# Attention in a two-layer encoder: head outputs in their own tile, causal entries by a select, bias rows loaded a head ahead

## The chip, the cores and the metric

The kernel runs on one core of a Trainium2 chip. The core has a matrix engine (TensorE, "PE" in the profile, with its weight loads shown apart as "PEld"), a vector engine (VectorE, DVE), a scalar engine (ScalarE, ACT), a general engine (GpSimd, POOL) and a sync engine (SP), which here does nothing but issue DMA transfers. Each engine works through a queue of its own in order, and the engines meet through semaphores. The metric is the device time of one execution in microseconds (us), as the median of several runs.

## The reference: what is computed

Two layers over 512 tokens of width 1024, in f32. Each layer adds to x a SwiGLU feed-forward, then a mixer, then a second feed-forward, each behind a norm with shift, scale and gate from a vector c. The mixer has three branches, and two of them are attention with eight heads of dimension 64:

```python
# branch A (group "a"): chunked, with a learned bias by clipped distance
logits = jnp.where(valid, logits + bias, NEG_INF)
# branch C (group "c"): frame-causal, with a forgetting bias
logits = einsum('bqhd,bkhd->bhqk', qb, kf) + (cq[..., None] - cum_k[:, :, None, :])
logits = jnp.where(kpos[None, :] <= qpos[:, None], logits, NEG_INF)
# both
p = jax.nn.softmax(logits, axis=-1);  out = p @ v
# the branches (B is an average pooling) are gated and merged
merged = jnp.sum(gates * branch, axis=2);  x = x + gate2 * (merged @ w_out)
```

## The kernel before

**Precision.** Products are made of three passes: each operand is split into a rounded high part (ScalarE copies, lines 277 and 384) and a low part (VectorE subtracts, lines 279 and 385), and TensorE adds high x high, high x low and low x high (lines 119 to 121).

**Attention, head by head.** `attention` runs over eight heads and, in each, over four row blocks of 128 queries. `logits` (from line 936) makes the scores of one row block against all keys up to its end in a PSUM tile "mm" (lines 942, 943). At line 946 VectorE adds the bias rows, writes the negated logits into a "t1" tile and keeps their minimum "mx". ScalarE takes the exponential (950) into a "t2" tile and the sum; VectorE takes the reciprocal (952), and POOL, or VectorE for the last row block, scales (954). Some products later `turn` transposes the probabilities on TensorE (966) and splits them into high and low parts (970 on ScalarE, 971 on VectorE). After every second row block `weigh` multiplies them with the values (988, 989) and finishes half a head's output: ScalarE copies one part from PSUM into a tile `yl` (992), VectorE adds the other part to it (993), ScalarE writes the high part (994), and POOL subtracts that from `yl` for the low part (995).

**The tiles in question.** Tiles of one tag share a fixed number of buffers. "t1" has two buffers, and `yl` is taken from it, as are the logits of line 946 and, in group c, the gates of the merge (line 1083). "strip" has two buffers of 128x768 and holds the bias rows; "ssum" has one of 128x512 and holds the bias rows of the last row block of group c. `cmask` is a constant 128x128 tile of 0 and -1e30, made at the start (lines 167 to 170).

**Bias rows.** `strip_a` (line 914) loads one head's learned bias, 256 KB, and clears a corner of it to -1e30 on POOL (917). `strip_c` (line 920) loads one head's forgetting bias for the first three row blocks into a "strip" tile (922) and for the last one into an "ssum" tile (924), each row broadcast to 128 partitions; POOL then adds `cmask` to the four diagonal blocks (928). Both are called at the start of a head, so in the written order a head's loads and all of its POOL steps stand ahead of its first logits.

**What fills TensorE meanwhile.** Between row blocks a filler yields projection products: in group a the query, key and value projections of group c (`proj_qk`, `proj_v`), in group c the gates and the branch product of branch A (`merge_units`). Their weights come in 512 KB loads on SP (line 266) into two "raw" buffers. Delayed steps, `turn` and `weigh` among them, are held as tasks with a due time counted in products, and run when that count is reached.

**Order.** The instructions are written in program order, but a planner lays each engine's queue out at build time: it follows its own estimates, prefers the instruction that stands earlier in the program, and lets a later one go first where the earlier one isn't ready by its estimate or waits for a buffer. The order that results is fixed, and the engines keep to it.

Of the kernel before, what the change touches and what calls it, by code (L numbers as in the profile page):

```python
# [15 lines left out]
F32 = mybir.dt.float32  # L16
# [3 lines left out]
ALU = mybir.AluOpType  # L20
AX = mybir.AxisListType

P = 128
T = 512
# [5 lines left out]
H = 8  # L30
HD = 64
NT = T // P
EPS = 1e-6
NEG = -1e30
BIG = 3.0e38
WINDOWS = (2, 4, 8, 16)
FVOFF = (0, 128, 384, 768)
# [3 lines left out]
def encoder_kernel(tc, xT, c, w_ada, b_ada, gains, w_gate, w_up, w_down, w_qkv, w_f, w_ubg,  # L41
                   qk_gain, rel, fbias, w_pool, pool_scale, w_branch, w_out, inv_cnt, w_first, out):
    nc = tc.nc
    pools = []

    def open_pool(**kw):
        p = tc.tile_pool(**kw)
        pools.append(p)
        return p.__enter__()

    cp = open_pool(name="consts", bufs=1)
# [8 lines left out]
    def nm(s):  # L60
        uid[0] += 1
        return f"{s}_{uid[0]}"

    def st(shape, dt, tag, bufs):
        return sb.tile(shape, dt, tag=tag, bufs=bufs, name=nm(tag))
# [4 lines left out]
    def mmt(shape=(P, T)):  # L70
        return ps.tile(list(shape), F32, tag="mm", bufs=4, name=nm("mm"))

    def blk(tag, dt=F32R):
        bufs = {"xv": 4, "v2": 4, "b": NB}[tag]
        return st([P, 2, T], dt, tag, bufs)

    def t1(cols=T):
        return st([P, cols], F32, "t1", 2)

    def t2(cols=T):  # L80
        return st([P, cols], F32, "t2", 3)
# [16 lines left out]
    def later(delay, fn, group=None):  # L98
        t = Task(pe[0] + delay, fn, group)
        tasks.append(t)  # L100
        return t

    def poll(everything=False, group=None):
        if polling[0]:
            return
        polling[0] = True
        while True:
            ready = [t for t in tasks if t.fn is None or everything or t.due <= pe[0]
                     or (group is not None and t.group == group)]
            if not ready:  # L110
                break
            t = min(ready, key=lambda z: z.due)
            tasks.remove(t)
            t.run()
        polling[0] = False
# [40 lines left out]
    for b, pc in enumerate(crows):  # L156
# [7 lines left out]
    fbc = cp.tile([H, L], F32, name="fbc")  # L164
    icnt = cp.tile([P, 4, 16], F32, name="icnt")

    cmask = cp.tile([P, P], F32, name="cmask")
    nc.gpsimd.memset(cmask, 0.0)
    nc.gpsimd.affine_select(cmask, cmask, pattern=[[-1, P]], base=0, channel_multiplier=1,
                            compare_op=ALU.is_ge, fill=NEG)  # L170
    qg8 = cp.tile([P, L, 4], F32, name="qg8")

    def late_inputs():
# [131 lines left out]
    HALF = T // 2  # L305
# [567 lines left out]
    def finish_turns(upto=3):  # L873

        for todo in turns:
            while len(todo) >= 4 - upto:
                todo.pop(0)()
# [33 lines left out]
        yield  # L911


    def strip_a(l, h):
        s = st([P, 768], F32, "strip", 2)
        nc.sync.dma_start(s[:, :T], rel[l, h])
        nc.gpsimd.memset(s[0:64, T - 64:T], NEG)
        return [s[:, T - (i + 1) * P:T] for i in range(NT)]

    def strip_c(l, h):  # L920
        s = st([P, 768], F32, "strip", 2)
        nc.sync.dma_start(s, fv_dram[l][h:h + 1, :768].broadcast_to([P, 768]))
        z = st([P, T], F32, "ssum", 1)
        nc.sync.dma_start(z, fv_dram[l][h:h + 1, 768:].broadcast_to([P, T]))
        r = [s[:, FVOFF[i]:FVOFF[i] + (i + 1) * P] for i in range(3)] + [z]
        for i in range(NT):
            dg = r[i][:, i * P:(i + 1) * P]
            nc.gpsimd.tensor_tensor(dg, dg, cmask, op=ALU.add)
        return r

    def attention(qs, ks, vs, strip, ys, filler, budget, group):


        open_pt = {}

        def logits(h, i, strips):
            p, off = divmod(h, 2)
            (q, ql), k = qs[p], ks[p]
            odd = h % 2
            n = (i + 1) * P  # L940
            s = mmt()
            mm(s[:, :n], q[:, odd, i * P:(i + 1) * P], k[:, odd, :n], start=True, stop=False)
            mm(s[:, :n], ql[:, odd, i * P:(i + 1) * P], k[:, odd, :n], start=False, stop=True)
            lg = t1(T)[:, :n]
            mx = st([P, 1], F32, "mx", 4)
            nc.vector.tensor_tensor_reduce(out=lg, in0=s[:, :n], in1=strips[i], scale=-1.0, scalar=BIG,
                                           op0=ALU.add, op1=ALU.min, accum_out=mx)
            pr = t2(T)[:, :n]
            sm = st([P, 1], F32, "sm", 4)
            nc.scalar.activation(pr, lg, AF.Exp, bias=mx, scale=-1.0, accum_out=sm)  # L950
            rs = st([P, 1], F32, "rs", 4)
            nc.vector.reciprocal(rs, sm)
            eng = nc.vector if i == NT - 1 else nc.gpsimd
            eng.tensor_scalar(pr, pr, rs, None, op0=ALU.mult)
            pe[0] += 0.5 * (i + 1.5)
            later(LAG_T, lambda: turn(h, i, pr), group)

        def turn(h, i, pr):
            half, c = divmod(i, 2)
            nj = 2 * half + 2  # L960
            if c == 0:
                open_pt[h] = st([P, 2, nj, 256], F32R, "ptb" if half else "pta", 2 if half else 1)
            pt = open_pt[h]
            tp = mmt()
            for j in range(i + 1):
                nc.tensor.transpose(tp[:, j * P:(j + 1) * P], pr[:, j * P:(j + 1) * P], ident)
            tv = tp[:, :(i + 1) * P].rearrange("p (j q) -> p j q", q=P)
            dh = pt[:, 0, :i + 1, c * P:(c + 1) * P]
            dl = pt[:, 1, :i + 1, c * P:(c + 1) * P]
            nc.scalar.copy(dh, tv)  # L970
            nc.vector.tensor_tensor(dl, tv, dh.bitcast(F32), op=ALU.subtract)
            pe[0] += 0.55 * (i + 1)
            if c == 1:
                later(LAG_V, lambda: weigh(h, half, pt), group)

        def weigh(h, half, pt):
            p, off = divmod(h, 2)
            rows = slice(off * HD, off * HD + HD)
            other = slice(HD - off * HD, 2 * HD - off * HD)
            if off == 0 and half == 0:  # L980
                ys.append(blk("b"))
            y = ys[p]
            o = mmt((P, HALF))
            nj = 2 * half + 2
            for j in range(nj):
                q0 = P if j == nj - 1 else 0
                v2 = vs[j][:, h, :, :].rearrange("p a d -> p (a d)")
                mm(o[:, q0:], v2, pt[:, 0, j, q0:], start=(j == 0), stop=False)
                mm(o[:, q0:], v2, pt[:, 1, j, q0:], start=False, stop=(j == nj - 1))
            cols = slice(half * HALF, (half + 1) * HALF)  # L990
            yl = t1(T)[:, :HALF]
            nc.scalar.copy(yl[rows, :], o[other, :])
            nc.vector.tensor_tensor(yl[rows, :], o[rows, :], yl[rows, :], op=ALU.add)
            nc.scalar.copy(y[rows, 0, cols], yl[rows, :])
            nc.gpsimd.tensor_tensor(y[rows, 1, cols], yl[rows, :], y[rows, 0, cols].bitcast(F32), op=ALU.subtract)
            pe[0] += 1.0 * nj

        for h in range(H):
            strips = strip(h)
            if group == "c":  # L1000
                finish_turns(h // 2)
            for i in range(NT):
                logits(h, i, strips)
                if i == NT - 1:
                    heads[0] = h + 1
                poll()
                goal = pe[0] + budget
                while filler is not None and pe[0] < goal:
                    if next(filler, "end") == "end":
                        filler = None  # L1010
                poll()
        if filler is not None:
            for _ in filler:
                pass
# [82 lines left out]
    class Mixer:  # L1097
# [10 lines left out]
        def run(self, nxt):  # L1108
# [15 lines left out]
            def fill_a():  # L1124
                yield from proj_qk(l, 3, g8[:, 2:3], True, qc)
                yield from proj_qk(l, 4, g[:, 3:4], False, kc)
                yield from proj_v(l, 5, "v2", vc)

            attention(qa, ka, va, lambda h: strip_a(l, h), ya, fill_a(), FILL_A, "a")
            heads[0] = H  # L1130

# [23 lines left out]
            def fill_c():  # L1155
                yield from merge_units(l, 0, ya, put_a)

            attention(qc, kc, vc, lambda h: strip_c(l, h), yc, fill_c(), FILL_C, "c")
            finish_turns()
            turns.clear()  # L1160
# [101 lines left out]
```

## Time and profile before

| | |
|---|---|
| median of 3 runs | 2403.73 us (2403.13 to 2406.02) |
| the profiled execution | 2404.73 us, span 2403.0 us |
| TensorE busy | 2359.9 us (98%) |
| VectorE busy | 1725.9 us (72%) |
| ScalarE busy | 1198.4 us (50%) |
| POOL busy | 351.7 us (15%) |
| attention, layer 0 | group a about 453 to 553 us from the span's start, group c about 553 to 665 us |
| attention, layer 1 | group a about 1637 to 1737 us, group c about 1737 to 1852 us |

The span is the time from the first to the last instruction in the profile; the device time of that execution is a little longer. A row of the form "engine line op out<-in" names a group of instructions by the engine and the line of the kernel that made them, with their output and inputs by tile name; t is "t1" or "t2", mm a PSUM tile. "DVE t L946 <- POOL b L995" in a table of waits says that VectorE stood idle before its instruction at line 946 until POOL's at line 995 was done. "SPq" is SP's queue.

### The profile page before, as it was taken

What the parts mean: (1) busy time and instruction counts of PE and PEld (TensorE: products, weight loads), DVE (VectorE), ACT (ScalarE), POOL (GpSimd) and SP (SyncE); (2) the same over time, 40 slices, a digit from 0 to 9 for tenths busy, and PEclk for the clock granted to TensorE, in tenths of its full rate; (3) what the DMA queues carried; (4) which work ended last, traced back from release to release, by engine and by line L of the source; (5) the groups of instructions that cost most, each with busy time, mean ns of one, the idle gap of its engine ahead of it and who ended that gap; (6) DMA issues with size and microseconds to landing.
All of it is one profiled execution on the core that took longest, in us unless ns stands there. A gap on an engine that the chain in (4) does not pass through costs nothing. (4 is left out here: it accounts for less than half of the span.)

```text
span 2403.0 us, 36815 instructions
## 1 busy us (share of the span) xinstructions
PE 2359.9 (98%) x14106; PEld 2085.6 (87%) x14106; DVE 1725.9 (72%) x3070; ACT 1198.4 (50%) x2090; POOL 351.7 (15%) x423
## 2 busy tenths in 40 slices
PE   7999999999999999999999999999999999999999
PEld 5799998778878898989998989978787788989898
DVE  8988866787665476878677878577866655658583
ACT  5353555786632353535553626466865324536252
POOL 3000011144432210000100000102444322000000
PEclk9999999999999999999999999999999999999999
DMA  7736342323345424353325353423233554223322
GB/s 274 238 113 228 99 152 84 93 79 109 108 171 201 175 98 166 105 186 105 132 83 196 104 197 106 141 79 98 80 116 108 193 182 169 71 97 106 101 96 103
DMA packets 116438, 320.94 MB, mean 134 GB/s; under 512 B 11139, under 2 KB 13315, under 8 KB 116261
## 3 DMA queue, kind: packets, MB, share of 16 engines
q1 hardware_dynamic: 115106, 314.38, 38.7%
q0 software_dynamic: 1152, 4.19, 0.4%
q8 instruction: 111, 1.82, 0.3%
q14 instruction: 67, 0.54, 0.1%
q10 hardware_dynamic: 2, 0.00, 0.0%
HBM read 312.16 MB, written 6.38 MB: 133 GB/s over the span
## 5 line engine op out<-in xcount | busy, mean ns | idle before, releaser
L277 ACT CAST whi<-raw 128x1024 fp32r<-128x1024 f32 (+1 forms) x267 | 277.4, 1043 | 431.5 <-PE acc L120 217.9
L279 DVE TENSOR_TENSOR wlo<-raw,whi 128x1024 fp32r<-128x1024 f32 x259 | 319.4, 1237 | 162.2 <-ACT whi L277 159.0
L119 PE MATMUL acc<-b,whi 128*128 128x512 f32 (+1 forms) x960 | 360.7, 376 | 0.2 <-DVE xv L434 0.2
L121 PE MATMUL acc<-b,wlo 128*128 128x512 f32 (+1 forms) x960 | 356.7, 372 | 1.8 <-DVE wlo L279 1.8
L120 PE MATMUL acc<-b,whi 128*128 128x512 f32 (+1 forms) x960 | 357.1, 372 | 0.0
L121 PEld LDWEIGHTS acc<-b,wlo 128*128 128x128 f32 x960 | 180.8, 188 | 34.0 <-DVE wlo L279 2.6
L119 PEld LDWEIGHTS acc<-b,whi 128*128 128x128 f32 x960 | 180.8, 188 | 31.8 <-DVE xv L434 0.6
L120 PEld LDWEIGHTS acc<-b,whi 128*128 128x128 f32 x960 | 181.0, 189 | 29.8
L119 PE MATMUL acc<-hhi,whi 128*128 128x512 f32 x480 | 191.3, 400 | 6.8 <-DVE b L1051 3.1
L121 PE MATMUL acc<-hhi,wlo 128*128 128x512 f32 x480 | 188.1, 393 | 1.0 <-DVE wlo L279 1.0
L120 PE MATMUL acc<-hlo,whi 128*128 128x512 f32 x480 | 188.6, 393 | 0.2 <-DVE hlo L711 0.2
L384 ACT CAST ptb<-v 128x1024 fp32r<-128x1024 f32 x128 | 134.0, 1050 | 97.7 <-DVE v L452 56.2
L385 DVE TENSOR_TENSOR ptb<-v,ptb 128x1024 fp32r<-128x1024 f32 x128 | 156.3, 1223 | 33.8 <-ACT ptb L384 32.3
L384 ACT CAST whi<-raw 128x1024 fp32r<-128x1024 f32 (+1 forms) x128 | 106.7, 834 | 92.1 <-PE acc L120 41.9
L119 PE MATMUL acc<-whi,hhi 128*128 128x512 f32 x336 | 137.8, 411 | 0.9 <-DVE xv L385 0.9
L206 DVE CUSTOM_DVE_ANT_0 v<-v,b,badac 128x1024 f32<-128x1024 f32 x96 | 127.1, 1333 | 15.0 <-DMA v<-in_w_ada_dram 14.8
L121 PE MATMUL acc<-whi,hlo 128*128 128x512 f32 x336 | 131.9, 393 | 0.0
L120 PE MATMUL acc<-wlo,hhi 128*128 128x512 f32 x336 | 131.6, 392 | 0.0
L385 DVE TENSOR_TENSOR wlo<-raw,whi 128x1024 fp32r<-128x1024 f32 (+1 forms) x128 | 121.6, 950 | 6.5 <-ACT whi L384 5.0
L434 DVE SCALAR_TENSOR_TENSOR xv<-acc,modc,xv 128x512 f32<-128x512 f32 (+1 forms) x112 | 77.3, 690 | 62.2 <-PE acc L121 62.0
L119 PEld LDWEIGHTS acc<-hhi,whi 128*128 128x128 f32 x480 | 90.6, 189 | 25.6 <-DVE b L1051 4.0
L329 POOL TENSOR_TENSOR ssum<-ssum,t 128x256 f32<-128x256 f32 (+1 forms) x45 | 46.5, 1034 | 442.8 <-ACT t L328 442.7
(315 smaller groups left out, 6667.5 us busy)
## 6 DMA issues: line engine op xcount, KB each, us to landing
v<-in_w_ada_dram SPq DMA_DIRECT2D x96, 512.0 KB, 5.3
raw<-in_w_down_dram SPq DMA_DIRECT2D x88, 512.0 KB, 3.7
raw<-in_w_up_dram SPq DMA_DIRECT2D x82, 512.0 KB, 4.0
raw<-in_w_gate_dram SPq DMA_DIRECT2D x79, 512.0 KB, 3.7
raw<-in_w_ubg_dram SPq DMA_DIRECT2D x56, 512.0 KB, 3.6
b<-in_w_ada_dram SPq DMA_DIRECT2D x48, 512.0 KB, 4.6
raw<-in_w_qkv_dram SPq DMA_DIRECT2D x42, 512.0 KB, 3.9
raw<-in_w_branch_dram SPq DMA_DIRECT2D x24, 512.0 KB, 3.7
```

Source lines behind the costliest of these rows:

```text
L119: mm(o, lh, rh, start=start, stop=False)
L120: mm(o, lh, rl, start=False, stop=False)
L121: mm(o, ll, rh, start=False, stop=stop)
L206: dot = nc.vector.tensor_tensor_reduce(out=raw, in0=raw, in1=silc[0], scale=1.0, scalar=badac[:, l, j, d:d + 1], op0=ALU.mult, op1=ALU.add ...
L277: nc.scalar.copy(hi, raw)
L279: lo_eng.tensor_tensor(lo, raw, hi.bitcast(F32), op=ALU.subtract)
L329: nc.gpsimd.tensor_tensor(self.ssum[:, cols], self.ssum[:, cols], q, op=ALU.add)
L384: nc.scalar.copy(hi, src)
L385: nc.vector.tensor_tensor(lo, src, hi.bitcast(F32), op=ALU.subtract)
L434: nc.vector.scalar_tensor_tensor(x, acc_j, gate, x, op0=ALU.mult, op1=ALU.add)
```

## The change

Three edits, all in attention:

- `yl` gets a tag of its own with one buffer of 128x256 (1 KB in each partition) in place of one of the two "t1" buffers.
- The constant tile `cmask` goes. Where POOL added it to a diagonal block, POOL's `affine_select` now keeps the entries at or below the diagonal and writes -1e30 into the others, in place.
- `strip_a` and `strip_c` become generators. `attention` starts the generator of the next head, which issues its load, ahead of the third row block of the present head, and of the first head ahead of the loop. At the start of a head the generator goes on with the POOL steps on the strip: the cleared corner in group a, three selects in group c. In group c the load of the last row block's rows is issued ahead of the first row block, and its select stands ahead of the last row block.

```diff
-    cmask = cp.tile([P, P], F32, name="cmask")
-    nc.gpsimd.memset(cmask, 0.0)
-    nc.gpsimd.affine_select(cmask, cmask, pattern=[[-1, P]], base=0, channel_multiplier=1,
-                            compare_op=ALU.is_ge, fill=NEG)
...
+    def causal(dg):
+        nc.gpsimd.affine_select(dg, dg, pattern=[[-1, P]], base=0, channel_multiplier=1,
+                                compare_op=ALU.is_ge, fill=NEG)
+
     def strip_a(l, h):
         s = st([P, 768], F32, "strip", 2)
         nc.sync.dma_start(s[:, :T], rel[l, h])
+        yield
         nc.gpsimd.memset(s[0:64, T - 64:T], NEG)
-        return [s[:, T - (i + 1) * P:T] for i in range(NT)]
+        r = [s[:, T - (i + 1) * P:T] for i in range(NT)]
+        yield r
+        yield r
+        yield r
 
     def strip_c(l, h):
         s = st([P, 768], F32, "strip", 2)
         nc.sync.dma_start(s, fv_dram[l][h:h + 1, :768].broadcast_to([P, 768]))
+        yield
+        r = [s[:, FVOFF[i]:FVOFF[i] + (i + 1) * P] for i in range(3)]
+        for i in range(3):
+            causal(r[i][:, i * P:(i + 1) * P])
+        yield r
         z = st([P, T], F32, "ssum", 1)
         nc.sync.dma_start(z, fv_dram[l][h:h + 1, 768:].broadcast_to([P, T]))
-        r = [s[:, FVOFF[i]:FVOFF[i] + (i + 1) * P] for i in range(3)] + [z]
-        for i in range(NT):
-            dg = r[i][:, i * P:(i + 1) * P]
-            nc.gpsimd.tensor_tensor(dg, dg, cmask, op=ALU.add)
-        return r
+        yield r
+        causal(z[:, 3 * P:])
+        yield r + [z]
...
-            yl = t1(T)[:, :HALF]
+            yl = st([P, HALF], F32, "yl", 1)
...
+        ahead = strip(0)
+        next(ahead)
         for h in range(H):
-            strips = strip(h)
+            mine, strips = ahead, next(ahead)
             if group == "c":
                 finish_turns(h // 2)
             for i in range(NT):
+                if i in (0, 3):
+                    strips = next(mine)
+                if i == 2 and h + 1 < H:
+                    ahead = strip(h + 1)
+                    next(ahead)
                 logits(h, i, strips)
```

## The prediction

> **What bounds the kernel now.** I read the page's head first, then a table of windows cut at the two attention stages of each layer, then the waits inside those windows, then the timeline round the longest TensorE (PE) gaps. The head:
>
> ```profile
> span 2403.0 us, 36815 instructions
> ...
> PE 2359.9 (98%) x14106; PEld 2085.6 (87%) x14106; DVE 1725.9 (72%) x3070; ACT 1198.4 (50%) x2090; POOL 351.7 (15%) x423
> ```
>
> PE is busy for all but 2403.0 - 2359.9 = 43.1 us, so the change pays only where PE stands still. It touches the attention stages alone. The windows are, in order, group a and group c of layer 0, then the same of layer 1 (columns: stretch, length, then busy time and instructions of PE, PEld, DVE, ACT, POOL, then clock and DMA):
>
> ```profile
> 453.00:553.00 100.00, 95.50 (x511) 78.27 (x510) 76.61 (x209) 75.60 (x172) 38.55 (x53) 1.00 0.28 83
> 553.00:665.00 112.00, 109.87 (x602) 92.55 (x601) 73.83 (x196) 70.00 (x170) 50.39 (x76) 1.00 0.36 115
> 1637.00:1737.00 100.00, 95.43 (x511) 78.25 (x510) 76.44 (x208) 75.23 (x169) 39.06 (x53) 1.00 0.28 84
> 1737.00:1852.00 115.00, 111.64 (x608) 93.44 (x607) 74.76 (x197) 71.22 (x174) 50.80 (x77) 1.00 0.35 112
> ```
>
> PE's idle time is 4.50 and 4.57 us in the two a windows, 2.13 and 3.36 in the two c windows: 14.6 us altogether. That is the ceiling of any gain, 0.6% of the span. POOL has half of each window free, so POOL time as such costs nothing; what counts is whom its waits hold up. The waits, again a, c, a, c (columns: total us, times, longest):
>
> ```profile
> PE mm L966 <- DVE t L993: 1.0, 1, 1.0
> PE mm L988 <- DVE mx L946: 0.5, 1, 0.5
> DVE t L946 <- POOL b L995: 0.9, 2, 0.6
> ```
> ```profile
> PE mm L966 <- DVE t L954: 1.3, 1, 1.3
> DVE t L946 <- POOL b L995: 7.8, 7, 1.4
> ```
> ```profile
> PE mm L966 <- DVE t L993: 1.0, 1, 1.0
> PE mm L988 <- DVE mx L946: 0.4, 1, 0.4
> DVE t L946 <- POOL b L995: 1.3, 2, 1.0
> ```
> ```profile
> PE mm L966 <- DVE t L954: 2.0, 2, 1.5
> DVE t L946 <- POOL b L995: 9.1, 7, 2.5
> ```
>
> The row "DVE t L946 <- POOL b L995" is the coupling that the change cuts. VectorE's logits step at L946 wants a "t1" buffer, one of two, and it is held by a head output whose last reader is POOL's subtraction at L995. It totals 0.9 + 7.8 + 1.3 + 9.1 = 19.1 us over the kernel, but nearly all of it lies in group c, where PE has projection products to do meanwhile.
>
> **The change, part by part.**
>
> *Head outputs in a tile of their own.* Where does the coupling reach PE? At the end of group c of both layers, and once in the middle of layer 1's:
>
> ```profile
> 656.30 0.41 DVE L971 TENSOR_TENSOR pta<-mm,pta 128x256 fp32r<-128x256 f32 x1
> 657.66 0.69 DVE L946 CUSTOM_DVE_ANT_0 t<-mm,ssum 128x512 f32<-128x512 f32 x1 [0.96 <-POOL b L995]
> ...
> 660.54 0.48 DVE L954 TENSOR_SCALAR t<-t,rs 128x512 f32<-128x512 f32 x1
> ```
> ```profile
> 661.17 0.63 PE L966 MATMUL mm<-ident,t 128*128 128x128 f32 x4 [1.33 <-DVE t L954]
> ```
> ```profile
> 1819.67 0.69 DVE L946 CUSTOM_DVE_ANT_0 t<-mm,ssum 128x512 f32<-128x512 f32 x1 [2.49 <-POOL b L995]
> ```
> ```profile
> 1843.58 0.69 DVE L946 CUSTOM_DVE_ANT_0 t<-mm,ssum 128x512 f32<-128x512 f32 x1 [0.96 <-POOL b L995]
> ```
> ```profile
> 1822.83 0.66 PE L966 MATMUL mm<-ident,t 128*128 128x128 f32 x4 [0.51 <-DVE t L954]
> ...
> 1847.08 0.63 PE L966 MATMUL mm<-ident,t 128*128 128x128 f32 x4 [1.50 <-DVE t L954]
> ```
>
> At 656.7 DVE stands still for 0.96 us with the last logits' matmul long done. Everything behind it (L946, the exponential, L954, the transposes of L966) is late by that, and PE waits 1.33 us. Without the coupling each end of c comes 0.96 us earlier: 2 x 0.96 = **1.9 us**. The 2.49 us at 1819.67 leaves PE only 0.51 us late, of which I take all: **0.5 us**. What is late next at the ends is the remaining 1.33 - 0.96 = 0.4 us, the length of the softmax chain itself.
>
> In the a windows the coupling shows on DVE for 0.9 and 1.3 us only. But two PE waits there are for buffers that a writer of "t1" frees (L993, which writes the head output, and L946): 1.0 + 0.5 and 1.0 + 0.4 = 2.9 us. Bounds: 0, if DVE and ACT, both busy for three quarters of those windows, are late there by themselves; 4.50 + 4.57 = 9.1, if all of a's PE idle time went. I take **2.9 us**, nearest to the rows that name these lines.
>
> The new tile has one buffer. A head output is begun by ACT at L992 and done with when L995 ends. The tightest spacing:
>
> ```profile
> 1710.70 0.74 POOL L995 TENSOR_TENSOR b<-t,b 64x256 fp32r<-64x256 f32 x1
> ```
> ```profile
> 1712.31 0.37 ACT L992 COPY t<-mm 64x256 f32<-64x256 f32 x1 [0.19 <-PE mm L989]
> ```
>
> The next L992 starts 1712.31 - 1711.44 = 0.87 us after the last L995 ended, so one buffer holds nobody up as long as L995 isn't later by more than that. Nothing for it in the sum. Bounds: 0 and rival 4. Queued behind a waiting L992 would be ACT's exponentials and weight casts.
>
> *Select in place of the mask add.*
>
> ```profile
> L928 POOL TENSOR_TENSOR strip<-strip,cmask 128x128 f32<-128x128 f32 x48 | 22.3, 492 | 13.7 <-DMA strip<-fv_dram 13.7
> ...
> L928 POOL TENSOR_TENSOR ssum<-ssum,cmask 128x128 f32<-128x128 f32 x16 | 7.4, 462 | 29.9 <-DMA ssum<-fv_dram 28.8 <-PE acc L121 1.1
> ...
> L169 POOL TENSOR_SCALAR_AFFINE_SELECT cmask<-cmask 128x128 f32<-128x128 f32 x1 | 0.3, 288 | 0.0
> ```
>
> The 64 adds take 22.3 + 7.4 = 29.7 us of POOL; 64 selects at the 288 ns of the one in this trace take 18.4. So 11.3 us of POOL go, with the mask's two start-up steps, and all of it lies beside PE work: **0**. The cover is POOL's free time in the c windows, (112 - 50.4) + (115 - 50.8) = 125.8 us; without it the 11.3 us would be the upper end. For a lower end I take each select at twice the longer mean, 2 x 492 ns: 63 us, 33 more than now, still under that cover. Nothing at either end.
>
> POOL's reads also collide with DVE, as the spread of L995 shows (first row: busy, mean ns, idle before; second: shortest, median, longest ns):
>
> ```profile
> L995 POOL TENSOR_TENSOR b<-t,b 64x256 fp32r<-64x256 f32 x64 | 51.9, 810 | 69.0 <-ACT b L994 68.0
> ```
> ```profile
> L995 POOL TENSOR_TENSOR b<-t,b x64: 725/737/1612, 471.2 to 1851.8; 64x256 fp32r<-64x256 f32 x64
> ```
>
> Some take twice the median; over all 64 the stretch is 64 x (810 - 737) ns = 4.7 us. With a single buffer for the head output a stretched L995 can hold ACT at the next L992, since 1612 - 737 = 875 ns is just the tightest gap of 0.87 us. That is rival 4. The Trainium skill, page "SBUF — State Buffer", section "Who interferes with whom", has a reason: a VectorE instruction with two SBUF inputs and a GpSimd instruction that reads SBUF use one read port, and whichever comes second waits for the whole of the first. By that rule the stretch doesn't go with the mask tile, because a select reads SBUF too; the sum by it would be the one of rival 4, the sum by the median L995 is mine.
>
> *Bias rows one head ahead.* The planner has done this already. SP issues each load as soon as the buffer of the head before last is free:
>
> ```profile
> 463.07 0.68 DVE L946 CUSTOM_DVE_ANT_0 t<-mm,strip 128x512 f32<-128x512 f32 x1
> ...
> 474.62 0.67 DVE L946 CUSTOM_DVE_ANT_0 t<-mm,strip 128x512 f32<-128x512 f32 x1
> ```
> ```profile
> 463.83 0.34 SPq L916 DMA_DIRECT2D strip<-in_rel_dram  x1
> ...
> 475.37 0.34 SPq L916 DMA_DIRECT2D strip<-in_rel_dram  x1
> ```
> ```profile
> SPq L916 <- DVE mx L946: 53.5, 12, 16.6
> ```
>
> The load follows the last logits of a head by 0.1 us (463.07 + 0.68 = 463.75, then 463.83), and its own first use comes only after the next head's last logits, 11.5 us later (474.62). There are still two buffers, so no load can start earlier. The 32 loads of strips and 16 of the fourth row block stay, in number and size. **0** for the loads. POOL's waits for these loads (13.7 and 28.8 us in the rows of the adds) hold L954 and L995 behind them. The clearing of a strip's corner (L917) and three of the four selects keep their place on POOL, ahead of the head's L954. The fourth row block's select moves from the head's start to its last row block, which may shorten the second; the t1 wait that such a wait passes on is counted already. What changes is rank on SP: in the written order the load stands two row blocks earlier, ahead of weight loads it used to follow.
>
> **Sum.** 1.9 + 0.5 + 2.9 = 5.3 us. The profiled execution took 2404.73 us (span 2403.0 and 1.7 around it), 1.0 above the median of 2403.73; the sum against it is 2399.4, and against the median 2398.4. I predict **2398.4 us**, 5.3 us or 0.22% faster. About 0.2%, 4.8 us, is what a measurement of this kernel can tell from no change, so this sits near the edge.
>
> **Rivals.**
> 1. *No measurable change*: only the ends of c gain, since a's PE waits come from ACT and DVE being full there. Then 2403.7 - 2.4 = 2401.3. For it: t1's waits in a are only 0.9 and 1.3 us, and PE in c is already 98% busy (109.87 of 112). Against it: the PE waits in a name L993 and L946.
> 2. *A larger gain*: the planner lays each engine's queue out anew from its own estimates, and a queue without the t1 coupling and with shorter POOL steps closes most of the 14.6 us. Three quarters of it: 2403.7 - 11 = 2393. For it: a's idle time is many small waits in one stretch. Against it: DVE and ACT do not get less to do.
> 3. *Slower*: the earlier rank of the strip load. SP is in order, and each strip load waits on L946, up to 16.6 us; weight loads now behind it come two row blocks later, about 2 x 3 us (a head of 12 us has four). It decides once that exceeds the lead of a weight load over its cast:
>
> ```profile
> 520.42 3.45 SPq L266 DMA_DIRECT2D raw<-in_w_qkv_dram  x2
> ```
> ```profile
> 526.09 1.05 ACT L277 CAST whi<-raw 128x1024 fp32r<-128x1024 f32 x1
> ```
> ```profile
> raw<-in_w_qkv_dram SPq DMA_DIRECT2D x42, 512.0 KB, 3.9
> ```
>
> The lead here is 526.09 - 520.42 - 3.9 = 1.8 us, so a load held for 6 us would stop PE for 4.2. One such load in each of the four stages costs 17 us less the 5.3: 2415. Against it: the wait's end, L946, is unchanged, and most weight loads wait for their own buffer longer.
> 4. *The one buffer*: ACT waits at L992 for a stretched L995, and the 4.7 us of stretch come back through the exponentials to PE: 2403.7 - 5.3 + 4.7 = 2403.1, no measurable change. For it: 875 ns against 870. Against it: that gap is the tightest; it takes both worst cases at one place.
>
> **How the numbers follow.** The forecast or the larger gain end faster by over 0.2%: I give the forecast 0.30 and rival 2 0.16, rival 1 0.26, rival 4 0.05, rival 3 0.23. That makes faster 0.46, same 0.31, slower 0.23. The forecast's own case runs from 2394 (half of a's 9.1 us more) to 2399. The whole range goes down to 2390, nearly the ceiling of 14.6 us, and up to 2412, most of rival 3.
>
> **What would show it.** In the profile after: no row "DVE t L946 <- POOL b L995"; PE's wait for L954 at the end of c at 0.4 us; the a windows with 1 to 2 us less idle each; selects at about 0.29 us; strip loads still issued right after L946. I am wrong if PE's new waits are on weight casts (rival 3), if ACT waits at L992 for L995, or if the a windows lose PE time because the queues were laid out differently.

## The result, and the profile after

The changed kernel takes 2398.68 us (median of 16 runs, 2396.68 to 2401.16), the kernel before, beside it on the same chip, 2403.62 us (16 runs, 2401.51 to 2406.57). The ratio is 0.998, with a 95% interval of 0.9974 to 0.9987. That is 4.9 us, or 0.2%, faster: the interval excludes no change, but reaches only 0.13% at its nearer end. Inside the attention stages the gain is all in group c, as the following views show.

In the profile after, line numbers have moved: before's 942, 946, 950, 954, 966, 970 and 971 are 950, 954, 958, 962, 974, 978 and 979 now; 988 and 989 are 996 and 997; 992 to 995 are 1000 to 1003; the learned strip's load is 917 (916), the forgetting strip's 927 (922), the select 911.

The head of the page of the changed kernel:

```profile
span 2397.4 us, 36848 instructions
...
PE 2359.3 (98%) x14106; PEld 2085.5 (87%) x14106; DVE 1724.6 (72%) x3070; ACT 1201.2 (50%) x2090; POOL 341.2 (14%) x421
```

The span is 5.6 us shorter, with TensorE as busy as before (2359.3 against 2359.9 us): what went is idle time. POOL lost 10.5 us (351.7 to 341.2), close to the 11.3 that the prediction worked out. The windows of the changed kernel, with the same columns as the prediction's (groups a and c of layer 0, then of layer 1):

```profile
453.00:553.00 100.00, 95.59 (x511) 78.30 (x511) 77.11 (x210) 75.76 (x172) 38.99 (x54) 1.00 0.27 83
553.00:665.00 112.00, 111.06 (x608) 93.69 (x607) 74.69 (x194) 72.56 (x172) 46.13 (x77) 1.00 0.34 115
1637.00:1737.00 100.00, 95.56 (x514) 78.34 (x513) 77.41 (x212) 75.06 (x171) 39.60 (x54) 1.00 0.28 84
1737.00:1852.00 115.00, 114.06 (x618) 96.06 (x617) 75.85 (x195) 73.71 (x173) 46.55 (x78) 1.00 0.36 114
```

TensorE's idle time is 4.41 and 4.44 us in the a windows, where it was 4.50 and 4.57: nothing to speak of. In the c windows it is 0.94 twice, where it was 2.13 and 3.36. The four windows together give 14.56 - 10.73 = 3.8 us, all but 0.2 of it in group c. Setting the start of the nth matmul of one trace beside that of the other places the 5.6 us of the span: nothing up to the end of layer 0's group a, 1.4 us in layer 0's group c, 3.1 us in layer 1's, and 1.3 us near 1907 us, in the feed-forward behind it. By this count group c gives 4.5 us, by its idle time 3.6; the record doesn't settle which is nearer.

Near 1907 us the trace of before has one late weight split that the trace of after lacks (last row of this section). It is no accident of this pair: all seven traces with the head output in its own tile lack it, and of the five traces with "t1" and the queues of before four have it, of 0.3 to 1.4 us. Why it goes isn't shown. One trace of before beside another also differs by up to 0.9 us in a stage, so the medians' 4.9 us are the better measure of the whole.

The waits of TensorE in the changed kernel, in the two windows of group a:

```profile
PE mm L827 <- DVE ptb L979: 1.1, 1, 1.1
PE mm L974 <- DVE yl L1001: 1.0, 1, 1.0
...
PE mm L996 <- DVE mx L954: 0.5, 1, 0.5
```
```profile
PE mm L827 <- DVE ptb L979: 1.1, 1, 1.1
PE mm L974 <- DVE yl L1001: 1.0, 1, 1.0
PE mm L950 <- DVE pta L979: 0.5, 1, 0.5
PE mm L996 <- DVE mx L954: 0.5, 1, 0.5
```

The two waits on which the prediction put its largest term, on the head output's sum (L1001, before L993) and on the logits' minimum (L954, before L946), stand there unchanged, 1.0 and 0.5 us, with the head output in its own tile. In group c of layer 1 one wait is left, and the same one in layer 0:

```profile
PE acc L119 <- ACT whi L273: 0.8, 1, 0.8
```

It was longer before, on the same step, then at L277:

```profile
PE acc L119 <- ACT whi L277: 1.2, 1, 1.2
```

The waits for the transposes' inputs in c (1.3 and 2.0 us before) are gone. VectorE had waited in 18 places for POOL's L995 before the step at L946, and the table of its waits has no such row now:

```profile
DVE t L946 <- POOL b L995: 19.0, 18, 2.5
```

A small new row stands in ScalarE's table (first block). SP's queue waited for group c's strips as in the second block before, and waits as in the third now:

```profile
ACT yl L1000 <- POOL b L1003: 1.9, 2, 0.9
```
```profile
SPq L922 <- DVE mx L946: 61.3, 16, 7.9
```
```profile
SPq L927 <- DVE mx L954: 78.0, 16, 7.5
SPq L917 <- DVE mx L954: 53.6, 12, 16.6
```

ScalarE meets the single buffer once in each layer, for 0.9 us. The strip loads still wait for the last logits of the head before, 12 and 16 times as before. Those of group c wait 78.0 us on SP in place of 61.3. Two thirds of the difference come from one load in each layer, which now stands ahead of a weight load and waits 6 us in place of 0.3. TensorE has no new wait on a weight cast: the 0.8 us on L273 were 1.2 us before.

The late weight split, in the waits of the kernel before between 1890 and 1915 us:

```profile
PE acc L121 <- DVE wlo L279: 1.0, 1, 1.0
```

### The profile page after: what moved, and what is told of

Same layout as the page of the kernel before. It is cut to its first block, busy times and chain, and to the rows that moved or that the text cites. A ratio compares the mean times of both kernels' runs of the same rounds, so it can differ in the third digit from the quotient of the medians.

```text
span 2397.4 us, 36848 instructions
## 1 busy us (share of the span) xinstructions
PE 2359.3 (98%) x14106; PEld 2085.5 (87%) x14106; DVE 1724.6 (72%) x3070; ACT 1201.2 (50%) x2090; POOL 341.2 (14%) x421
## 4 chain that ended last, share of the span: by engine, by line
PE 83%; DVE 7%; ACT 5%; issue 2%; DMA 1%; POOL 1%; SPq 0%; DVEq 0%; ACTq 0%; POOLq 0%
PE acc L119 14%; PE acc L121 14%; PE acc L120 14%; PE acc L128 4%; PE mm L129 4%; PE mm L128 4%; PE mm L130 4%; PE acc L129 4%; PE acc L130 4%; PE mm L119 4%; PE mm L120 4%; PE mm L121 4%; POOL strip L1048 1%; DVE v L202 1%; ACT b L836 1%
## 5 line engine op out<-in xcount | busy, mean ns | idle before, releaser
L273 ACT CAST whi<-raw 128x1024 fp32r<-128x1024 f32 (+1 forms) x267 | 277.4, 1043 | 427.9 <-PE acc L120 226.1
L275 DVE TENSOR_TENSOR wlo<-raw,whi 128x1024 fp32r<-128x1024 f32 x259 | 319.5, 1237 | 159.4 <-ACT whi L273 156.6
L202 DVE CUSTOM_DVE_ANT_0 v<-v,b,badac 128x1024 f32<-128x1024 f32 x96 | 127.6, 1339 | 17.0 <-DMA v<-in_w_ada_dram 16.7
L119 PE MATMUL mm<-hhi,whi 128*128 128x512 f32 x280 | 109.5, 392 | 1.4 <-ACT whi L273 1.4
```

The costliest lines, as they stand in the source:

```text
L119: mm(o, lh, rh, start=start, stop=False)
L202: dot = nc.vector.tensor_tensor_reduce(out=raw, in0=raw, in1=silc[0], scale=1.0, scalar=badac[:, l, j, d:d + 1], op0=ALU.mult, op1=ALU.add ...
L273: nc.scalar.copy(hi, raw)
L275: lo_eng.tensor_tensor(lo, raw, hi.bitcast(F32), op=ALU.subtract)
```

## The experiments

Two theories stood against each other at the start. By the one, the prediction's, the gain comes from the tile: what counts is who holds the "t1" buffer. By the other it comes from POOL: a shorter step there lets L995 run sooner, and the tile adds nothing. Each ratio below is against runs of the kernel before on the same chip, with its 95% interval. A queue that is called the same has its instructions in the same order in the trace.

### The loads a head ahead, alone

The edit stands against the changed kernel: its generators stay, and the mask tile, the adds and the head output in "t1" come back.

```diff
+    cmask = cp.tile([P, P], F32, name="cmask")
...
-        nc.gpsimd.affine_select(dg, dg, ...)
+        nc.gpsimd.tensor_tensor(dg, dg, cmask, op=ALU.add)
...
-            yl = st([P, HALF], F32, "yl", 1)
+            yl = t1(T)[:, :HALF]
```

> The kernel before with the generators alone: bias loads and the POOL steps written where the changed kernel has them, mask tile and adds kept, head outputs in t1. Theory A (the loads already went a head ahead, so this edit does nothing): the order of every queue is that of before, the ratio is 1.000 within 0.001, the waits DVE t L946 <- POOL b L995 still total about 19 us. Theory B (the earlier loads carry the gain): ratio 0.998, about 5 us less.

Measured: 2402.29 us, ratio 0.9992 (0.9983 to 1.0001). The queue of every engine is the one of before, instruction for instruction: the planner had hoisted these loads already. The wait remains:

```profile
DVE t L957 <- POOL b L1006: 18.9, 18, 1.5
```

Between 18.9 and the 19.0 us of before there is no difference. This part of the change does nothing. As a second trace of the same queues it also shows the scatter: TensorE's idle time in the c windows is 2.64 and 2.70 us, where the first had 2.13 and 3.36, nearly the same sum.

### The selects, alone

```diff
-    cmask = cp.tile([P, P], F32, name="cmask")
...
-            nc.gpsimd.tensor_tensor(dg, dg, cmask, op=ALU.add)
+            nc.gpsimd.affine_select(dg, dg, pattern=[[-1, P]], base=0, channel_multiplier=1,
+                                    compare_op=ALU.is_ge, fill=NEG)
```

> The kernel before with the mask tile gone and the 64 adds turned into selects, nothing else. Theory A (POOL time lies beside other work): ratio 1.000 within 0.001, POOL about 11 us less busy, selects at about 0.29 us each, PE's gap ahead of the last transposes of group c still 1.3 to 1.7 us. Theory B (shorter POOL steps free t1 earlier): the waits of L946 on the subtraction fall by a third or more and 1 to 2 us go.

Measured: 2399.96 us, ratio 0.9982 (0.9974 to 0.9991). The selects alone, with the head output still in "t1", give most of the gain; the prediction had priced them at nothing. Their rows, the wait and the two c windows:

```profile
L924 POOL TENSOR_SCALAR_AFFINE_SELECT strip<-strip 128x128 f32<-128x128 f32 x48 | 14.7, 337 | 12.3 <-DMA strip<-fv_dram 12.3
L924 POOL TENSOR_SCALAR_AFFINE_SELECT ssum<-ssum 128x128 f32<-128x128 f32 x16 | 4.7, 294 | 31.1 <-DMA ssum<-fv_dram 25.8 <-DVE t L990 4.2 <-ACT xv L380 0.6
```
```profile
DVE t L943 <- POOL b L992: 12.6, 18, 0.9
```
```profile
553.00:665.00 112.00, 110.67 (x606) 93.21 (x605) 74.65 (x196) 70.76 (x171) 46.15 (x76) 1.00 0.38 115
...
1737.00:1852.00 115.00, 113.56 (x618) 95.56 (x617) 76.30 (x195) 72.75 (x172) 48.13 (x78) 1.00 0.36 112
```

VectorE still waits for POOL in 18 places, but 12.6 us in place of 19.0 and never over 0.9. TensorE's idle time in the c windows is 1.33 and 1.44 us. Its wait for the last transposes' input, 1.3 and 1.5 us at the two ends of c before, is 0.6 in each layer:

```profile
PE mm L963 <- DVE t L951: 0.6, 1, 0.6
```

Every queue has the order of before, but for the two start-up steps of the mask tile that POOL no longer has. So it is the length of POOL's steps that makes this gain, not another order.

### The tile and the selects, without the early loads

```diff
-    cmask = cp.tile([P, P], F32, name="cmask")
...
-            nc.gpsimd.tensor_tensor(dg, dg, cmask, op=ALU.add)
+            nc.gpsimd.affine_select(dg, dg, ...)
...
-            yl = t1(T)[:, :HALF]
+            yl = st([P, HALF], F32, "yl", 1)
```

> Own tile for the head outputs, and selects (the own tile does not fit beside the mask tile); loads and POOL steps written as before, no generators. Theory A (the own tile is the whole gain): 2398 to 2399 us, ratio 0.998, the same as the changed kernel, no wait of L946 on the subtraction, PE's gap ahead of the last transposes of group c at 0.3 us in both layers. Theory B (part of the gain is the loads): 2400 to 2402 us.

Measured: 2399.18 us, ratio 0.9976 (0.9966 to 0.9986). Every queue has the order of the changed kernel, and the c windows have its busy time, 111.06 and 114.06 us. The tile takes 0.39 + 0.50 us more of idle time out of them than the selects alone; the two medians, 2399.96 and 2399.18, are 0.8 us apart with intervals that overlap, so the time doesn't resolve it. The tile comes with another order: VectorE's, ScalarE's, TensorE's and SP's queues are no longer those of before, and no run has the tile with the old order. Nor does one have the tile with the adds kept; the doubled selects of the next section, longer than an add, come nearest to it.

### The selects doubled, in "t1" and in a tile of its own

If POOL's time in group c counts because "t1" waits for it, doubling the selects must cost with the one buffer and not with the other. Selecting twice changes no value.

```diff
+            nc.gpsimd.affine_select(dg, dg, ...)
             nc.gpsimd.affine_select(dg, dg, ...)
```

With the head output in "t1":

> The kernel with selects alone (head outputs in t1, no generators), each select issued twice, which leaves the result as it is: about 0.6 us of POOL per diagonal block, against 0.46 us of the add and 0.3 us of one select. Theory A (selects gained because POOL's step stands ahead of the head output's subtraction on POOL, and so holds the t1 buffer): the gain of the select is lost, 2404 to 2407 us, waits of L943 on the subtraction at 19 us or more against 12.6 with one select. Theory B (the select gained through something else, such as the start-up or the port): 2400 us as with one select.

Measured: 2409.04 us, ratio 1.0021 (1.0012 to 1.003): slower than before, and 9.1 us over the median of one select, which ran on another chip; the two ratios give 9.4 us.

With the whole change:

> The changed kernel with each select issued twice: POOL per diagonal block again longer than the add, head outputs in their own tile. Theory A (the own tile and the cheap select cut the same coupling, so with the own tile POOL's time does not matter): 2398 to 2400 us, at most 1 us above the changed kernel, and 4 us or more below the same selects without the own tile. Theory B (the gain is the selects' alone): 2404 us or more.

Measured: 2398.79 us, ratio 0.9974 (0.9964 to 0.9983): as the changed kernel. In both, every queue keeps the order that it has with single selects. The wait and the c windows of the first:

```profile
DVE t L945 <- POOL b L994: 22.3, 18, 1.7
```
```profile
553.00:665.00 112.00, 108.53 (x590) 90.45 (x588) 74.07 (x195) 70.31 (x171) 53.05 (x105) 1.00 0.35 109
...
1737.00:1852.00 115.00, 111.03 (x602) 91.93 (x601) 74.81 (x200) 71.22 (x175) 55.43 (x111) 1.00 0.33 105
```

and those of the second:

```profile
553.00:665.00 112.00, 111.06 (x609) 93.64 (x608) 75.14 (x196) 72.26 (x172) 54.11 (x106) 1.00 0.36 115
...
1737.00:1852.00 115.00, 114.06 (x616) 96.00 (x615) 76.04 (x196) 73.46 (x172) 54.86 (x107) 1.00 0.37 115
```

POOL does the same 105 to 111 instructions in 53 to 55 us in all four. With "t1" TensorE is idle for 3.47 and 3.97 us, with the tile for 0.94 and 0.94, just as with single selects. So with "t1" POOL's time reaches TensorE, and the row that names the way, L994 freeing a "t1" buffer for VectorE, is gone with the own tile. The tile, with the order that the planner lays for it, makes POOL's time immaterial, at least up to twice the selects; how much of that is the order isn't told apart.

### No step on the diagonal at all

The kernel before without the mask tile and its adds; the causal mask of group c is left out of the computation.

```diff
-            nc.gpsimd.tensor_tensor(dg, dg, cmask, op=ALU.add)
+            pass
```

> The kernel before without mask tile and without adds: POOL has no step on a diagonal block at all, so future keys are attended to in group c (that part of the computation is left out). Head outputs in t1. Theory A (the time falls with POOL's step per diagonal block, through the subtraction that stands behind it and the t1 buffer it frees): below the 2400 us of one select, 2396 to 2399 us, with the waits of L941 on the subtraction at 6 to 10 us. Theory B (one select was already hidden): 2400 us.

Measured: 2399.98 us, ratio 0.998 (0.9971 to 0.9989), what one select takes (2399.96). VectorE's wait:

```profile
DVE t L942 <- POOL b L991: 11.5, 16, 0.9
```

Together the runs with the head output in "t1" give a dose curve: with each step more, the time that POOL spends on a diagonal block grows, and all four kernels have the same queues but for these steps. With no step, VectorE waits 11.5 us for the subtraction and the kernel takes 2400.0 us; with a select of about 0.3 us, 12.6 and 2400.0; with an add of 0.46 to 0.49 us, 19.0 and about 2404; with two selects of 0.3 us, 22.3 and 2409. It is flat up to a point between one select and one add, and then steep. That fits a slack in group c which a select stays inside and an add overruns; the runs show the knee, not what sets its place. The 11.5 us that are left without any step belong to the head output's own chain: POOL's idle time before L991 there ends with ScalarE's L990, in 98.5 of 98.7 us.

### The head output in "t2"

```diff
-            yl = t1(T)[:, :HALF]
+            yl = t2(T)[:, :HALF]
```

> The kernel before with the head outputs taken from the three t2 buffers in place of the two t1 buffers; mask tile, adds and loads as before. Theory A (it is the coupling through t1 that cost, not the want of a tile): the waits of L946 on the subtraction go, PE's gap at the end of group c falls to about 0.3 us, 2398 to 2400 us. Theory B (any tile shared with the softmax couples the same way): the probabilities' scaling on POOL and the exponential wait in its place, 2402 to 2406 us.

Measured: 2416.69 us, ratio 1.005 (1.0037 to 1.0063): slower. Now the exponential, which writes "t2", waits for the subtraction (first row), and layer 0's group a loses most:

```profile
ACT t L950 <- POOL b L995: 33.2, 28, 2.7
```
```profile
453.00:553.00 100.00, 91.97 (x475) 74.25 (x474) 73.14 (x193) 70.93 (x156) 36.91 (x47) 0.98 0.27 77
```

TensorE is idle for 8.0 us there, where it was 4.5. The clock column of this row reads 0.98: just behind a wait of TensorE of 2.6 us its granted clock was 0.5 for 3.4 us, which by estimate costs 1.7 us:

```profile
PE mm L831 <- DVE ptb L971: 2.6, 1, 2.6
```
```profile
545.88:549.29 3.41, 3.41 (x13) 2.95 (x12) 1.86 (x4) 2.23 (x4) 1.24 (x1) 0.50 0.00 0
```

Layer 1's group a ends with such a wait too, but no drop of the clock stands behind it. By the nth matmul that stage is 5.2 us longer than before and layer 0's 6.6 us, so the drop is the smaller part. The queues have another order here too, and the run doesn't say how much of the loss is that. The coupling to a buffer ring is not worth the same everywhere: in "t1" it holds VectorE in group c, in "t2" it holds ScalarE in group a too.

### The subtraction done twice, with the whole change

```diff
             nc.gpsimd.tensor_tensor(y[rows, 1, cols], yl[rows, :], y[rows, 0, cols].bitcast(F32), op=ALU.subtract)
+            nc.gpsimd.tensor_tensor(y[rows, 1, cols], yl[rows, :], y[rows, 0, cols].bitcast(F32), op=ALU.subtract)
```

> The changed kernel with the subtraction on POOL that ends a head output's life issued twice, so that the one buffer is held about 0.75 us longer, 64 times. Theory A (the single buffer has room): up to 1 us more than the changed kernel, waits of ACT L1000 on the subtraction below 10 us. Theory B (the single buffer is at its limit, the tightest gap was 0.87 us): 3 us or more above the changed kernel, with ACT's waits there passed on to PE.

Measured: 2402.21 us, ratio 0.9989 (0.998 to 0.9998), some 3 us over the changed kernel. This frees the own tile some 0.74 us later each time. ScalarE's wait at L1000, and the a windows:

```profile
ACT yl L1000 <- POOL b L1004: 3.5, 2, 1.8
...
ACT t L958 <- POOL b L1004: 2.9, 5, 0.6
```
```profile
453.00:553.00 100.00, 94.38 (x503) 77.02 (x502) 77.67 (x205) 74.65 (x168) 46.39 (x64) 1.00 0.29 83
...
1637.00:1737.00 100.00, 94.35 (x502) 76.94 (x501) 77.79 (x205) 74.05 (x166) 45.63 (x62) 1.00 0.30 84
```

The wait for the own tile only went from 1.9 to 3.5 us, in the same two places. Every queue has the order of the changed kernel. What is lost is lost in group a (idle 5.62 and 5.65 us against 4.41 and 4.44), and the c windows keep their 111.06 and 114.06. The second row names a cause that isn't the tile: POOL's longer occupancy itself, ahead of a "t2" buffer. The run doesn't tell the two apart for group a. It does show that one buffer is enough in group c even with a release 0.74 us later.

### What bounds group a

Three runs of the changed kernel went after the 4.4 us of idle time that group a kept. `Q_GATE` and `K_GATE` say after how many heads the turns of group c's queries and keys may start.

```diff
-    Q_GATE, K_GATE = (2, 2, 4, 4), (6, 6, 8, 8)
+    Q_GATE, K_GATE = (2, 3, 4, 5), (6, 7, 8, 8)
```

> The changed kernel with the transposes of group c's queries and keys released one pair of heads per head (from heads 2, 3, 4, 5 and 6, 7, 8, 8 on) in place of two at once (2, 2, 4, 4 and 6, 6, 8, 8); same work. Theory A (PE's 4.4 us of idle time in each group a window come from ACT and VectorE being full while two of these stand together): the a windows lose 1 to 3 us of idle time each, 2393 to 2397 us. Theory B (they come from the head-output chain itself): 2398 to 2399 us, a windows unchanged.

```diff
-    Q_GATE, K_GATE = (2, 2, 4, 4), (6, 6, 8, 8)
+    Q_GATE, K_GATE = (4, 4, 5, 5), (6, 6, 8, 8)
```

> The changed kernel with the query transposes released from heads 4, 4, 5, 5 on in place of 2, 2, 4, 4; same work. Theory A (four of these turns in a row make the idle time of group a, between 498 and 511 us in layer 0): the gaps there spread or fall, each a window 0.5 to 2 us less idle, 2395 to 2398 us. Theory B (the turns only move): within 1 us of the changed kernel, idle time of the a windows at 4 to 5 us.

```diff
-                    nc.scalar.activation(low, pt[own, :], AF.Identity, scale=gc)
+                    nc.vector.tensor_scalar(low, pt[own, :], gc, None, op0=ALU.mult)
```

> The changed kernel with the second copy of group c's rounded queries (L839, eight per layer, 0.68 us each on ScalarE) made by VectorE from the same PSUM tile. Theory A (in group a PE waits for PSUM buffers that come free late because ScalarE's queue is full there, which no head-output tile can help): each a window loses 1 to 2 us of its 4.4 us of idle time, 2395 to 2397 us. Theory B (VectorE is as full as ScalarE): the a windows keep their idle time or gain some, 2398 to 2402 us.

Measured: 2400.29 (0.9984, 0.9975 to 0.9993) for the spread turns, 2399.36 (0.998, 0.997 to 0.9989) for the later ones, 2399.41 (0.998, 0.9972 to 0.9989) for the copy on VectorE. None is below the 2398.68 of the changed kernel. The a window of layer 0, of the later turns and then of the copy on VectorE:

```profile
453.00:553.00 100.00, 96.17 (x510) 78.13 (x509) 76.41 (x208) 75.85 (x171) 38.28 (x53) 1.00 0.28 83
```
```profile
453.00:553.00 100.00, 96.22 (x512) 78.83 (x511) 83.13 (x216) 69.59 (x160) 38.12 (x51) 1.00 0.29 84
```

Both take about 0.6 us of idle time out of this window (3.83 and 3.78 against 4.41), and the time doesn't move by what could be measured. Less idle time isn't yet a shorter stage. By the nth matmul, group a of either layer is 0.8 us shorter than in the changed kernel with the copy on VectorE, but 0.1 to 0.2 us longer with the later turns. There are 16 such copies in a layer, not eight as expected; moving them takes 6 us of ScalarE's time in this window and adds 6 to VectorE's. With the copy moved, the wait for the head output's sum is still there:

```profile
PE mm L827 <- DVE ptb L979: 1.1, 1, 1.1
PE mm L974 <- DVE yl L1001: 1.1, 1, 1.1
```

So ScalarE's load isn't what makes that wait, though by the count of matmuls it has a share in the others. The later turns replace these rows by others (1.3 us for the query's own splitting step at L842): the stall moves with the work. The spread turns also give other queues, and the a windows are idle for 4.69 us each, 0.3 more than in the changed kernel. What bounds group a stays open.

## Why the prediction was right, and where it wasn't

The time forecast, 2398.4 us, is 0.3 us from the measured median, and the sum of 5.3 us stands against 4.9. That it comes so near is luck: group a gave 2.7 us less than forecast, group c 1.2 more, and 1.3 came in the feed-forward near 1907 us, where nothing was forecast.

- **The coupling at the ends of c, 1.9 us, and in layer 1's c, 0.5: right in mechanism, too small.** The c windows gave 1.2 and 2.4 us, 3.6 in all against 2.4. The 0.5 us in layer 1 went as forecast. Of what was not forecast, 0.4 us is the wait on a weight cast there, 1.2 us before and 0.8 after, and 0.2 a wait of L942 on L946. The forecast left 0.4 us of waiting at each end; the profile after has no TensorE wait there that its table of waits names. In the timeline of the changed kernel the last transposes come 0.52 us after the product before them began, where the products around stand about 0.23 apart, so some 0.3 us is left:

```profile
657.24 0.45 PE L119 MATMUL acc<-hhi,whi 128*128 128x512 f32 x1
657.52 0.40 PE L120 MATMUL acc<-hlo,whi 128*128 128x512 f32 x1
658.04 0.66 PE L974 MATMUL mm<-ident,t 128*128 128x128 f32 x4
```

  The planner has also put these transposes some eight products earlier in TensorE's queue. I had them where they were; with the selects alone, where they stand as before, 0.6 us is left at each end.
- **Group a, 2.9 us: the step that failed.** The prediction took two waits of TensorE there for the coupling's doing, since a writer of "t1" ends each. Both stand unchanged in the profile after. That the instruction which ends a wait writes into a shared buffer ring doesn't say that it was late for that buffer. The prediction's own row of VectorE's waits, 0.9 and 1.3 us in the a windows, was the better bound, and rival 1 used it. Inside the attention stages its mechanism (only c gains) is what happened, though c gave 3.6 us where it allowed 2.4.
- **The select at 0: right on top of the tile, wrong in its reason.** With the tile, POOL's steps can be twice as long at no cost (2398.79 us). But alone the select gives 2399.96 us, nearly the whole gain. The cover that the prediction named, POOL's 125.8 us of free time in group c, was an average; what counted was the short stretch in which L995 stands in the queue behind the strip's steps and a "t1" buffer stands behind L995. The size of the operation was right for the fourth block (294 ns against 288) and low for the strips (337, in the run with the selects alone). The tile and the select are two ways to one gain, not two terms of a sum: the selects alone bring about 4 us of it, the tile makes the selects' length immaterial.
- **The loads a head ahead at 0: right,** and for the reason given: the planner had them there. Rival 3's condition didn't arise. SP's queue differs by four swaps of neighbours between the two kernels; the run without the early loads has them too, so they come with the tile. The group c strips wait 16.7 us more in it, and no weight cast was late for that.
- **Rival 4, the one buffer:** ScalarE does wait at L1000 for L1003, twice, 1.9 us in all, which the prediction had named as a sign of being wrong. TensorE's rows in the c windows, where both waits fall, show nothing of it. Nor is it a stretched subtraction that ScalarE waits for: the two took 814 and 819 ns, 0.08 us over the median. The stretch itself is still there: the longest L1003 is 1612 ns, as the longest L995 was, and the mean went from 810 only to 788 ns, that is (788 - 735) x 64 = 3.4 us of stretch in place of 4.7. The four longest, 1484 to 1612 ns, each began while VectorE ran a 128x1024 weight subtraction (L275, 1.22 us), which reads two tiles in SBUF. The Trainium skill, page "SBUF — State Buffer", section "Who interferes with whom", has the rule that a VectorE instruction with two SBUF inputs contends with a GpSimd instruction that reads SBUF; the trace agrees.

```profile
L1003 POOL TENSOR_TENSOR b<-yl,b x64: 723/735/1612, 471.3 to 1846.4; 64x256 fp32r<-64x256 f32 x64
```
```profile
L1003 POOL TENSOR_TENSOR b<-yl,b 64x256 fp32r<-64x256 f32 x64 | 50.4, 788 | 70.7 <-ACT b L1002 69.9
```

Of the marks that the prediction set, the missing row for L946 and the strip loads' place came out. The selects came out at 294 to 343 ns rather than 0.29 us. The a windows' gain of 1 to 2 us each did not come: 0.1 us each.

## What to carry to other kernels

A mostly idle engine is not a free one: ask what stands in its queue behind the step in question, and which buffer that next instruction frees. Before a wait is credited to a buffer, look for the row that names the buffer's holder; that the late instruction writes such a buffer is not enough. Where two edits cut the same chain, price each alone and the pair once, since their gains do not add up.

## What had not been expected of the hardware

A GpSimd select of 128x128 f32 in place took 294 to 343 ns as a mean of its groups, against 462 to 492 ns for the add of a 128x128 mask tile. The difference, 0.15 us in 64 instructions of an engine busy for 14% of the span, was worth about 4 us where a shared buffer waited behind it. With the head output in its own tile even a second select for each block cost nothing that could be measured (2398.79 against 2398.68 us).
